# A 16-byte gap between the row tiles of the split weights in the feature-wise projections

## The chip, the cores and the metric

The kernel runs on one core of one Trainium2 chip. The metric is the device time of one execution in microseconds (us), here the median of three runs. All data are 32-bit floats. The core's engines are TensorE (PE in the profile; its weight loads stand apart as PEld), VectorE (DVE), ScalarE (ACT), GpSimd (POOL) and SyncE (SP, which here only starts transfers). SBUF is the on-chip memory, seen as 128 partitions; an address below is always a byte within a partition.

## The reference, cut to what matters

The program computes a two-layer encoder trunk for 256 tokens of width 2048. Each layer normalises its input, multiplies it by one wide input matrix, runs two groups of mixers on the parts (mLSTM and Mamba-2 in the first layer, sparse attention and gated delta rule in the second) and multiplies the result by an output matrix:

```python
D_MODEL, SEQ = 2048, 256
def layer_ab(x, norm_g, w_in, ..., w_out):
    h = rms_norm(x, norm_g)
    proj = jnp.einsum('btd,de->bte', h, w_in)          # the projections in question
    q, k, v, o_pre, z_a, i_pre, f_pre, z_b, xbc, dt_raw = split_cols(proj, SPLIT_AB)
    y_a = mlstm_branch(...)
    y_b = mamba2_branch(...)
    y = jnp.concatenate([y_a, y_b], axis=-1)
    return x + jnp.einsum('bte,ed->btd', y, w_out)
```

The second layer has the same form with other mixers. Most of the work is these matrix products with a weight that is read once from HBM.

## The kernel before, in words

**Three products for one.** A matrix is split into a rounded part and a rest: activations into `hi` and `lo`, weights into `wh` (a cast by ACT, line 254) and `wl` (raw weights minus `wh`, by DVE, line 255). A product is then `hi*wh + lo*wh + hi*wl`, three TensorE instructions in the one-pass type float32r that add up in one PSUM bank.

**Blocks of weights.** Weights come 512 columns wide, in groups of four row tiles of 128 rows (`KG = 4`). One transfer of 1 MB brings a group into a buffer `wr`; ACT and DVE split it in two halves of two row tiles each into `wh` and `wl` (`load_w`). In these buffers a row tile's 512 columns take 2048 bytes, and the next row tile follows at once: the four tiles of a group lie 2048 bytes apart. The buffers have 64 elements more than they need (`PAD`), and `SHIFT` says how many elements after the buffer's start the data begin: 8 or 24 for products with `hT`, 32 or 48 with `cT`, 0 with the units `ua`, `ub`, `uc`; the first of two is for token-wise, the second for feature-wise products.

**Two ways to multiply.** In `proj_tok` (tiles `pt`) the activations are the stationary operand and 512 weight columns stream past them. In `proj_feat` (tiles `pf`) the weights are the stationary operand, 128 columns at a time (block `b`), and 256 tokens stream past. The streamed operand is a row tile of `hT` (16 tiles of 512 elements: 256 `hi`, then 256 `lo`), or of `cT` for the products with `w_uk`. In the first three groups of a feature-wise projection the row tile `k` is the outer loop and the four blocks `b` the inner one, so 12 instructions use one row tile; in the last group it is the other way round, and the row tile changes every 3 instructions. A projection of 512 columns has 4 groups of 48 instructions; there are 36 of them with `hT`, and 4 of one group each with `cT`. Between row tiles `tick()` puts a few instructions of the mixers into TensorE's order.

**Places in SBUF.** In the built program every row tile of `hT` begins 192 bytes past a multiple of 256, and every row tile of `wh` and `wl` for a feature-wise product with `hT` begins on a multiple of 256. `cT` begins at 32 and its weights at 96. Take the start of the stationary operand minus the start of the streamed one, modulo 256, and call it the offset: it is 64 for all feature-wise products, in every row tile and block (blocks are 512 bytes apart, the `hi` and `lo` halves 1024). For all token-wise products it is 0. One other set of products matters below, the numerators `num` of the mLSTM heads: there `v` streams past `Ph` and `Pl`, 512 columns a time. `Ph` and `Pl` begin at 192; `v` begins at 192 in the even heads and at 96 in the odd ones, since the two are in different buffers. So the offset is 0 in even heads and 96 in odd ones.

Of the kernel before, what the change touches and what calls it, by code (L numbers as in the profile page):

```python
# [9 lines left out]
F32R = mybir.dt.float32r  # L10
# [19 lines left out]
KG, WR, WS = 4, 3, 2  # L30


PAD, SHIFT = 64, {"h": (8, 24), "c": (32, 48), "u": (0, 0)}


APART, APART_DG, APART_SP, SPARE = 56, 72, 72, 16
# [34 lines left out]
def trunk(ctx, tc, x, rel_bias, ab_norm, ab_w_in, ab_ml_b_i, ab_ml_b_f, ab_ml_norm, ab_ssm_conv_w,  # L71
# [21 lines left out]
    ab_w_in, ab_w_out, cd_w_in, cd_w_out = ab_w_in[0], ab_w_out[0], cd_w_in[0], cd_w_out[0]  # L93
# [4 lines left out]
    wp = ctx.enter_context(tc.tile_pool(name="wp", bufs=3))  # L98
# [12 lines left out]
    pin = tc.keep_in_program_order  # L111
# [80 lines left out]
    def pump():  # L192

        for gen in list(bg):
            if next(gen, "end") == "end":
                bg.remove(gen)
# [14 lines left out]
    def scaled_to(n):  # L211

        while scaling["done"] < n:
            next(scaling["gen"], None)
            scaling["done"] += 1

    def tick():

        if scaling["wait"] is not None and scaling["done"] < 8:
            scaling["wait"] -= 1  # L220
            if scaling["wait"] <= 0:
                scaled_to(scaling["done"] + 1)
                scaling["wait"] = 2
        ticking.append(True)
        beat[0] += 1
        for track in (steps, side):
            if track and (track is steps or not steps or beat[0] % 2) and next(track[0], "end") == "end":
                track.pop(0)
        ticking.clear()
# [8 lines left out]

    spare = []

    def load_w(src, r0, nk, pieces, n, shift, pin=lambda ins: ins, pool=None):


        pump()
        if spare:
            spare.append(spare.pop(0))
            pool = spare[0]
        wr = raw_w(src, r0, nk, pieces, n)
        wh, wl = parts_w(n, shift, pool)
        with tc.high_priority():  # L250
            m = nk // 2 if n == 512 else nk
            for k in range(0, nk, m):
                ks = slice(k, k + m)
                pin(A.copy(wh[:, ks, 0:n], wr[:, ks, 0:n]))  # L254
                pin(V.tensor_tensor(wl[:, ks, 0:n], wr[:, ks, 0:n], wh[:, ks, 0:n].bitcast(F32), op=OP.subtract))  # L255
        return wh, wl

    def raw_w(src, r0, nk, pieces, n, parts=None, after=()):

        wr = wp.tile([128, KG * 512], F32, name="wr", tag="wr", bufs=WR).rearrange("p (k n) -> p k n", n=n)  # L260
        if sum(m for _, m, _ in pieces) < n:
            G.memset(wr[:, 0:nk, 0:n], 0.0)
        k = 0
        for m in parts or [nk]:
            for c0, nc_, at in pieces:
                nc.sync.dma_start(wr[:, k:k + m, at:at + nc_], src[r0 + k * 128:r0 + (k + m) * 128, c0:c0 + nc_].rearrange("(k p) n -> p k n", p=128))
            k += m
            if after:
                after.pop()()
        return wr  # L270

    def parts_w(n, shift, pool=None):
        return [(pool or wp).tile([128, KG * 512 + PAD], F32R, name=name, tag=name, bufs=1 if spare and pool else WS)[:, shift:shift + KG * 512].rearrange("p (k n) -> p k n", n=n)
                for name in ("wh", "wl")]

    def token_part(pt, X, w, k, nk, t, cs, begun=False):
# [10 lines left out]
    def proj_tok(src, r0, X, c0, n=512, loads=(), begun=None):  # L287

        pts = begun or two_banks()
        nk = len(X)  # L290
        shift = SHIFT[X[0][0].name[0]][0]

        def part(pt, w, k, t):
            token_part(pt, X, w, k, nk, t, slice(0, n), begun and t == 0)

        for g in range(0, nk, KG):

            w = loads[g // KG] if loads else load_w(src, r0 + g * 128, KG, [(c0, n, 0)], n, shift)
            if g + KG == nk and not loads:
                order = [(k, t) for t in range(2) for k in range(KG)]  # L300
            else:
                order = [(k, t) for k in range(KG) for t in range(2)]
            for i, (k, t) in enumerate(order):
                part(pts[t], w, g + k, t)
                if i % 2:
                    tick()
        return pts

    def proj_feat(src, r0, X, pieces, loads=(), raw=False):


        n = max(p[2] + p[1] for p in pieces)
        n = (n + 127) // 128 * 128
        nb = n // 128
        pts = [ps.tile([128, 512], F32, name=f"pf{b}", tag="pt") for b in range((nb + 1) // 2)]
        nk = len(X)
        shift = SHIFT[X[0][0].name[0]][1]
        kg = KG * 512 // n
        for g, m in [(g, min(kg, nk - g)) for g in range(0, nk, kg)]:
            wh, wl = loads[g // kg] if g // kg < len(loads) else load_w(src, r0 + g * 128, m, pieces, n, shift)  # L320
            last = g + m == nk
            order = [(k, b) for b in range(nb) for k in range(m)] if last else [(k, b) for k in range(m) for b in range(nb)]
            for at, (k, b) in enumerate(order):
                xt, i = X[g + k]
                if xt is hT and not raw:
                    scaled_to(i // 2 + 1)
                bs = slice(b * 128, b * 128 + 128)
                pt = pts[b // 2][:, b % 2 * 256:b % 2 * 256 + 256]
                PE.matmul(pt, wh[:, k, bs], xt[:, i, 0:256], start=g + k == 0 and b % 2 == 0, stop=False)
                PE.matmul(pt, wh[:, k, bs], xt[:, i, 256:512], start=False, stop=False)  # L330
                PE.matmul(pt, wl[:, k, bs], xt[:, i, 0:256], start=False, stop=last and k == m - 1 and (b % 2 == 1 or b == nb - 1))
                if at % nb == nb - 1:
                    tick()
        return pts
# [144 lines left out]
    def first_input(pool, loads, c0, shift):  # L479
# [48 lines left out]
        def part(k, m):  # L528

            g, ks = k // 4, slice(k % 4, k % 4 + m)  # L530
            if len(loads) == g:
                loads.append(parts_w(512, shift))
            wh, wl = loads[g]
            with tc.high_priority():
                pin(A.copy(wh[:, ks], raw[g][:, ks]))  # L535
                pin(V.tensor_tensor(wl[:, ks], raw[g][:, ks], wh[:, ks].bitcast(F32), op=OP.subtract))  # L536
# [113 lines left out]
    with ExitStack() as st:  # L650
# [5 lines left out]
        pts = proj_tok(ab_w_in, 0, X, AV, loads=first_w, begun=begun)  # L656
        v_first = mp.tile([128, 2, 512], F32, name="v_first")
        bc_cols = lambda i: [(AXBC + 2048 + i * 512, 512, 0)]
        bc_w = [load_w(ab_w_in, 0, KG, bc_cols(0), 512, SHIFT["h"][1], pin)]
        for t in range(2):  # L660
            A.activation(v_first[:, t], pts[t], AF.Copy, scale=rs_x[:, t:t + 1])

# [5 lines left out]
        def bc_half(i):  # L668
            pts = proj_feat(ab_w_in, 0, X, bc_cols(i), () if i else bc_w)
            if not taps:  # L670
                taps.append(columns("xconv", [(rows(ab_ssm_conv_w[0, k]), 24) for k in range(4)] + [(rows(ab_ssm_conv_b[0]), 24)], mp, mp, nc.gpsimd))
            xconv = taps[0]
            for b in range(2):
                V.tensor_tensor(pair(pts[b]), pair(pts[b]), rb2, op=OP.mult)
                conv_gate(pts[b], xconv, 16 + i * 4 + b * 2, 24, xconv[:, 96:120], BC[:, i * 4 + b * 2:i * 4 + b * 2 + 2].rearrange("p b t -> p (b t)"))
# [88 lines left out]
        cd_ = dp.tile([4, 256], F32, name="cd_")  # L764
        ad_ = dp.tile([32, 256], F32, name="ad_")
        steps.append(gates(proj_feat(ab_w_in, 0, X, [(AI, 4, 0), (AFG, 4, 28), (ADT, 32, 32)])))
        bc_half(1)

        with sps:
# [107 lines left out]
            for g in range(4):  # L877

                pts = proj_feat(ab_w_in, 0, X, [(AXBC + g * 512, 512, 0)])
                flush()  # L880
                steps.extend(turns)
                turns.clear()
                xf = []
                for b in range(2):
                    xf.append(sp.tile([128, 512], F32, name="xf", tag="xf", bufs=2))
                    V.tensor_tensor(pair(pts[b]), pair(pts[b]), rb2, op=OP.mult)
                    conv_gate(pts[b], xconv, g * 4 + b * 2, 24, xconv[:, 96:120], xf[b])
                zb = sp.tile([128, 2, 512], F32, name="zb", tag="zb", bufs=ZB)
                gated = []
                steps.append(heads(g, xf, zb, gated, decays(g + 1) if g < 3 else lag(LE)))  # L890
                pts = proj_tok(ab_w_in, 0, X, AZB + g * 512)
                for t in range(2):
                    gate2(zb[:, t], pts[t], rsh[:, t:t + 1])
                gated.append(True)
# [143 lines left out]
    with ExitStack() as st:  # L1038
# [17 lines left out]
        for i in range(2):  # L1056
            pts = proj_feat(cd_w_in, 0, X, [(CIQ + i * 512, 512, 0)], raw=i == 0)
            for b in range(2):
                src = pair(pts[b])
                if i == 0:  # L1060
                    tm = kq.tile([128, 768], F32, name="tm", tag="tm", bufs=2)
                    src = tm[:, 0:512].rearrange("p (k t) -> p k t", k=2)
# [715 lines left out]
```

## Time and profile before

| | |
|---|---|
| median of 3 runs | 2044.75 us (2044.51 to 2045.87) |
| profiled execution, its own time | 2042.25 us |
| its span, first to last instruction | 2040.5 us |
| TensorE busy | 99% of the span, 13143 instructions |
| VectorE, ScalarE, GpSimd busy | 72%, 53%, 6% |
| TensorE's granted clock | 0.999 of full speed |
| chain that ended last | TensorE 98%: `pt` 47%, `pf` 40% |

A matmul's duration in the profile includes its way through the array, which overlaps with the next one: `pf` instructions last 280 ns but start about 113 ns after each other. So busy time tells little here, and the spacing from start to start is what counts. It is read from the timeline (start, duration, instruction, count) or from the chain of waits, whose pieces give a start, a length and a count: length over count is the time of one instruction.

### The profile page before, as it was taken

To read this page: it belongs to the slowest core of one execution; us is meant where nothing else is said; L and a number is where in the kernel's file an instruction comes from. 1 tells how busy PE (TensorE), PEld (TensorE's weight loads), DVE (VectorE), ACT (ScalarE), POOL (GpSimd) and SP (SyncE) were. 2 spreads that over 40 slices of the span, in tenths; PEclk is the share of its full clock that TensorE was granted. 3 is DMA by queue.
4 is the path that set the end of the run, shared out by engine and by line. 5 is a ranking of instruction groups with operands and counts; after the bars stand their busy time and mean duration, and the time that the engine had idled before them with its cause. 6 is when DMAs were issued, how large, how long until landed. Compare 5 with 4: busy or idle time off the path is not lost.

```text
span 2040.5 us, 32857 instructions
## 1 busy us (share of the span) xinstructions
PE 2027.8 (99%) x13143; PEld 1834.2 (90%) x13143; DVE 1478.2 (72%) x2459; ACT 1086.9 (53%) x1803; POOL 115.3 (6%) x188
## 2 busy tenths in 40 slices
PE   9999999999999999999999999999999999999998
PEld 8999998888889888999998888999999999999986
DVE  5998875555555566789699996556577767877776
ACT  6466644444434445567644444666466556555654
POOL 2000001000000000012210000000000000000001
PEclk9999999999999999999999999999999999999999
DMA  7655454656556565569966669565655555555543
GB/s 246 230 200 190 168 168 167 217 180 195 181 188 209 175 204 184 169 218 277 270 196 213 222 209 308 197 207 180 218 199 186 188 192 196 189 181 193 175 176 124
DMA packets 239434, 407.32 MB, mean 200 GB/s; under 512 B 42813, under 2 KB 68417, under 8 KB 238321
## 3 DMA queue, kind: packets, MB, share of 16 engines
q1 hardware_dynamic: 232432, 383.67, 56.5%
q0 software_dynamic: 4560, 18.15, 2.9%
q10 hardware_dynamic: 2288, 3.41, 0.5%
q8 instruction: 103, 1.69, 0.3%
q14 instruction: 51, 0.41, 0.1%
HBM read 388.26 MB, written 20.06 MB: 200 GB/s over the span
## 4 chain that ended last, share of the span: by engine, by line
PE 98%; DVE 1%; ACT 0%; DMA 0%; issue 0%; SPq 0%; DVEq 0%; ACTq 0%
PE pt L83 47%; PE pf L83 40%; PE pt_last L83 1%; PE py L83 1%; PE turn L87 1%; PE pu L83 1%; PE pog L83 1%; PE pq L83 1%; PE lgt L83 1%; PE po L83 1%; PE pn L83 0%; PE num L83 0%; DVE wl L255 0%; PE pw L83 0%; PE si L83 0%; PE xt L87 0%
## 5 line engine op out<-in xcount | busy, mean ns | idle before, releaser
L255 DVE TENSOR_TENSOR wl<-wr,wh 128x1024 fp32r<-128x1024 f32 x657 | 780.9, 1230 | 352.5 <-ACT wh L254 352.3
L254 ACT CAST wh<-wr 128x1024 fp32r<-128x1024 f32 x657 | 656.2, 1047 | 510.8 <-PE pt L83 253.7
L83 PE MATMUL pf<-hT,wh 128*128 128x256 f32 x4640 | 817.2, 280 | 0.0
L83 PEld LDWEIGHTS pf<-hT,wh 128*128 128x128 f32 x4640 | 704.5, 188 | 4.1 <-issue 1.9
L83 PE MATMUL pf<-hT,wl 128*128 128x256 f32 x2320 | 644.5, 278 | 0.0
L83 PE MATMUL pt<-wh,hT 128*128 128x512 f32 x1600 | 506.0, 392 | 0.0
L83 PEld LDWEIGHTS pf<-hT,wl 128*128 128x128 f32 x2320 | 436.5, 188 | 0.0
L83 PEld LDWEIGHTS pt<-wh,hT 128*128 128x128 f32 x1600 | 300.7, 188 | 61.9 <-ACT wh L535 0.5
L83 PE MATMUL pt<-wl,hT 128*128 128x512 f32 x800 | 312.4, 391 | 0.2 <-DVE wl L536 0.2
L83 PE MATMUL pt<-wh,uc 128*128 128x512 f32 x704 | 230.8, 399 | 0.0
L83 PEld LDWEIGHTS pt<-wl,hT 128*128 128x128 f32 x800 | 150.5, 188 | 31.0 <-DVE wl L536 1.5
L83 PEld LDWEIGHTS pt<-wh,uc 128*128 128x128 f32 x704 | 132.2, 188 | 25.9
L83 PE MATMUL pt<-wl,uc 128*128 128x512 f32 x352 | 138.2, 393 | 0.0
L637 DVE SCALAR_TENSOR_TENSOR cy<-pf,gconv,cy 128x255 f32<-128x255 f32 (+2 forms) x192 | 91.0, 479 | 7.8 <-ACT cy L633 5.0
L591 DVE TENSOR_TENSOR xr<-pt,xr 128x512 f32<-128x512 f32 x76 | 52.3, 688 | 41.5 <-PE pt L83 41.5
L83 PE MATMUL pt<-wh,ua 128*128 128x512 f32 x256 | 80.2, 393 | 0.0
L83 PE MATMUL pt<-wh,ub 128*128 128x512 f32 x256 | 79.2, 389 | 0.0
L83 PEld LDWEIGHTS pt<-wl,uc 128*128 128x128 f32 x352 | 66.4, 189 | 12.1
L83 PEld LDWEIGHTS pt<-wh,ub 128*128 128x128 f32 x256 | 48.1, 188 | 10.0
L83 PEld LDWEIGHTS pt<-wh,ua 128*128 128x128 f32 x256 | 47.9, 188 | 9.5
L633 ACT ACTIVATE cy<-pf,gconv 128x256 f32<-128x256 f32 x64 | 30.0, 469 | 47.2 <-DVE cy L637 35.6
L1576 POOL TENSOR_TENSOR QD<-QD,qm 128x256 f32<-128x256 f32 x32 | 27.2, 882 | 484.6 <-DVE qm L1571 275.2
(543 smaller groups left out, 2002.8 us busy)
## 6 DMA issues: line engine op xcount, KB each, us to landing
wr<-in_cd_w_in_dram SPq DMA_DIRECT2D x140, 1024.0 KB, 5.1
wr<-in_ab_w_in_dram SPq DMA_DIRECT2D x86, 1024.0 KB, 4.9
wr<-in_cd_w_out_dram SPq DMA_DIRECT2D x48, 1024.0 KB, 5.1
wr<-in_ab_w_out_dram SPq DMA_DIRECT2D x32, 1024.0 KB, 5.1
wr<-in_ab_w_in_dram SPq DMA_DIRECT2D x35, 512.0 KB, 4.5
zd<-zk SPq DMA_DIRECT2D x12, 512.0 KB, 6.7
Dt<-gd POOLq DMA_DIRECT2D x8, 512.0 KB, 6.4
wr<-in_cd_w_uk_dram SPq DMA_DIRECT2D x4, 1024.0 KB, 5.3
```

The source lines that it names most:

```text
L83: return held(nc.tensor.matmul(*args, **kw))
L87: return held(nc.tensor.transpose(*args, **kw))
L254: pin(A.copy(wh[:, ks, 0:n], wr[:, ks, 0:n]))
L255: pin(V.tensor_tensor(wl[:, ks, 0:n], wr[:, ks, 0:n], wh[:, ks, 0:n].bitcast(F32), op=OP.subtract))
L591: V.tensor_tensor(xc, pt, xc, op=OP.add)
L633: A.activation(yi, u, AF.Copy, scale=tap(3))
L637: V.scalar_tensor_tensor(yi[:, s:256], u[:, 0:256 - s], tap(3 - s), yi[:, s:256], op0=OP.mult, op1=OP.add)
L1576: G.tensor_tensor(QD[:, h], QD[:, h], qm[:, h // 2 * 256:h // 2 * 256 + 256], op=OP.mult)
```

## The change

Where a feature-wise projection is 512 columns wide, the row tiles of `wh` and `wl` are laid 516 elements apart instead of 512, by a new parameter `apart = 4` (16 bytes) of `load_w` and `parts_w`. Row tile 0 stays where it was; row tiles 1, 2 and 3 begin 16, 32 and 48 bytes later than before. The buffers keep their size (48 bytes fit into `PAD`) and their places, and no other tile moves. ACT's cast and DVE's subtraction now write two rows of 512 elements with a gap instead of 1024 in a row, and DVE reads `wh` so. The gate projection (128 columns wide), `proj_narrow` and all token-wise products keep their layout. Every engine's instructions stay in the same order; nothing is added, removed or moved.

```diff
-PAD, SHIFT = 64, {"h": (8, 24), "c": (32, 48), "u": (0, 0)}
+APART_K, PAD, SHIFT = 4, 64, {"h": (8, 24), "c": (32, 48), "u": (0, 0)}
...
-    def load_w(src, r0, nk, pieces, n, shift, pin=lambda ins: ins, pool=None):
+    def load_w(src, r0, nk, pieces, n, shift, pin=lambda ins: ins, pool=None, apart=0):
...
-        wh, wl = parts_w(n, shift, pool)
+        wh, wl = parts_w(n, shift, pool, apart)
...
-    def parts_w(n, shift, pool=None):
-        return [(pool or wp).tile([128, KG * 512 + PAD], F32R, name=name, tag=name, bufs=1 if spare and pool else WS)[:, shift:shift + KG * 512].rearrange("p (k n) -> p k n", n=n)
+    def parts_w(n, shift, pool=None, apart=0):
+        pitch = n + apart
+        return [(pool or wp).tile([128, KG * 512 + PAD], F32R, name=name, tag=name, bufs=1 if spare and pool else WS)[:, shift:shift + KG * 512 // n * pitch].rearrange("p (k n) -> p k n", n=pitch)[:, :, 0:n]
                 for name in ("wh", "wl")]
...
-            wh, wl = loads[g // kg] if g // kg < len(loads) else load_w(src, r0 + g * 128, m, pieces, n, shift)
+            wh, wl = loads[g // kg] if g // kg < len(loads) else load_w(src, r0 + g * 128, m, pieces, n, shift, apart=APART_K if n == 512 else 0)
...
-        bc_w = [load_w(ab_w_in, 0, KG, bc_cols(0), 512, SHIFT["h"][1], pin)]
+        bc_w = [load_w(ab_w_in, 0, KG, bc_cols(0), 512, SHIFT["h"][1], pin, apart=APART_K)]
```

## The prediction, made before the result

> **What bounds the kernel now.** I read the engines' shares and the chain of waits first.
>
> ```profile
> span 2040.5 us, 32857 instructions
> PE 2027.8 (99%) x13143; PEld 1834.2 (90%) x13143; DVE 1478.2 (72%) x2459; ACT 1086.9 (53%) x1803; POOL 115.3 (6%) x188
> PE 98%; DVE 1%; ACT 0%; DMA 0%; issue 0%; SPq 0%; DVEq 0%; ACTq 0%
> ```
>
> The chain that sets the end is TensorE for 98%, so only what changes the spacing of its instructions counts. The profiled execution took 2042.25 us, 1.75 us more than its span; the median is 2044.75 us, 4.25 us above the span. I work in the span and carry the difference over to the median.
>
> Next the chain in order of time, in its long unbroken pieces (start, us, what, count), and the timeline of one place:
>
> ```profile
> 1028.43 53.12 PE pf L83 x468
> 1081.55 174.10 PE pt L83 x768
> 1255.65 28.07 PE pf L83 x240
> 2008.94 22.08 PE pt_last L83 x120
> ```
>
> A feature-wise instruction costs 53.12/468 = 113.5 ns, a token-wise one 174.10/768 = 226.7 ns: twice the streamed columns, twice the time. So 113.3 ns is the pace of streaming 256 columns, and there is no room below it that the trace shows. But the piece at 1255.65 costs 28.07/240 = 117.0 ns. The timeline shows where its 192 instructions with `hT` (a whole projection) begin, where the 48 with `cT` begin, and what follows them:
>
> ```profile
> 1255.49 0.40 PE L83 MATMUL pf<-hT,wh 128*128 128x256 f32 x2
> ...
> 1278.10 0.41 PE L83 MATMUL pf<-cT,wh 128*128 128x256 f32 x2
> ...
> 1283.56 0.40 PE L83 MATMUL pt<-wh,cT 128*128 128x512 f32 x1
> ```
>
> The 192 go at 22.61/192 = 117.8 ns, the 48 at 5.46/48 = 113.8, with the same shape and offset (64). So feature-wise products know two paces, and can stay in one for a whole projection. The row of `pt_last` shows that the offset also plays a part: its 72 instructions of 512 columns at 226.7 ns take 16.3 us, which leaves 5.8 us for 48 of 256 columns at offset 0, or 120 ns each.
>
> How much time the slow pace takes now I counted from the starts of neighbouring `pf` instructions: of 6980 pairs, 5518 lie under 116 ns (mean 113.3), 1330 between 116 and 130 (mean 117.9), the rest have something between them. The first of the 1330 and the last:
>
> ```profile
> 33.11 0.40 PE L83 MATMUL pf<-hT,wh 128*128 128x256 f32 x2
> 33.35 0.28 PE L83 MATMUL pf<-hT,wl 128*128 128x256 f32 x1
> 33.47 0.40 PE L83 MATMUL pf<-hT,wh 128*128 128x256 f32 x2
> ...
> 1925.36 0.48 PE L83 MATMUL pf<-hT,wh 128*128 128x256 f32 x2
> 1925.68 0.28 PE L83 MATMUL pf<-hT,wl 128*128 128x256 f32 x1
> ```
>
> Three instructions from 33.11 to 33.47 are 0.36 us, 118 ns apiece after rounding. In all 1330 x (117.9 - 113.4) = 6.0 us: all that a better layout can win back.
>
> **The change part by part.** No instruction is added, removed or moved on any engine, so no wait, transfer or queue changes its place. Two things change: patterns that ACT and DVE write, and the offset between the operands of feature-wise products.
>
> *The patterns.* ACT's cast and DVE's subtraction write two rows of 512 instead of 1024 in one. The trace has no such pair with and without a gap at this size, but has one at half of it: `hT` is written as two rows of 256 with a gap of 256 (lines 424 and 423), `vf` as 512 in a row (lines 639 and 638).
>
> ```profile
> L255 DVE TENSOR_TENSOR wl<-wr,wh 128x1024 fp32r<-128x1024 f32 x656 | 778.6, 1228 | 348.6 <-ACT wh L254 348.3
> L639 DVE SCALAR_TENSOR_TENSOR vf<-vf,cy 128x512 f32<-128x512 f32 x16 | 11.0, 685 | 0.0
> L424 DVE TENSOR_TENSOR hT<-xg,hT 128x512 fp32r<-128x512 f32 x16 | 10.5, 688 | 0.9 <-ACT hT L423 0.9
> ...
> L254 ACT CAST wh<-wr 128x1024 fp32r<-128x1024 f32 x656 | 654.3, 1046 | 507.3 <-PE pt L83 253.7 <-PE pf L83 117.0 <-issue 94.9
> L638 ACT ACTIVATE vf<-cy 128x512 f32<-128x512 f32 x16 | 10.0, 627 | 6.0 <-DVE cy L637 6.0
> L423 ACT CAST hT<-xg 128x512 fp32r<-128x512 f32 x16 | 9.2, 618 | 8.8 <-DVE xg L436 5.6 <-DVE xg L462 3.1
> ```
>
> 688 against 685 ns on DVE, 618 against 627 on ACT: nothing, on the path or off it. Were it 5% (60 ns on each of 296 halves, 18 us on DVE), it would be hidden too: the 48 instructions of a group last 48 x 113.3 = 5.4 us, splitting the next group takes DVE 2 x 1.228 = 2.5 us and ACT 2.1, and ACT's idle time before its casts mostly ends when TensorE lets go of a buffer. With that cover gone it would be the 18 us.
>
> *The offset.* 37 times 192 = 7104 feature-wise instructions are 512 columns wide (`cT`'s included), 1776 for each row tile. Row tile 0 stays at offset 64, the others go to 80, 96 and 112. The trace has no row at 80 or 112, but it has 96: the numerators of the odd mLSTM heads, beside the even heads at offset 0, same instructions, same code. First two places of an odd head, then an even one:
>
> ```profile
> 325.11 0.63 PE L83 MATMUL num<-v,Ph 128*128 128x512 f32 x2
> 325.57 0.39 PE L83 MATMUL num<-v,Pl 128*128 128x512 f32 x1
> 325.80 0.40 PE L83 MATMUL pt<-wh,hT 128*128 128x512 f32 x1
> ...
> 327.17 0.63 PE L83 MATMUL num<-v,Ph 128*128 128x512 f32 x2
> 327.64 0.39 PE L83 MATMUL num<-v,Pl 128*128 128x512 f32 x1
> 327.87 0.63 PE L83 MATMUL num<-v,Ph 128*128 128x512 f32 x2
> 328.34 0.40 PE L83 MATMUL num<-v,Pl 128*128 128x512 f32 x1
> 328.58 0.39 PE L83 MATMUL pt<-wh,hT 128*128 128x512 f32 x1
> ...
> 454.52 0.62 PE L83 MATMUL num<-v,Ph 128*128 128x512 f32 x2
> 454.98 0.39 PE L83 MATMUL num<-v,Pl 128*128 128x512 f32 x1
> 455.20 0.62 PE L83 MATMUL num<-v,Ph 128*128 128x512 f32 x2
> 455.66 0.39 PE L83 MATMUL num<-v,Pl 128*128 128x512 f32 x1
> 455.88 0.39 PE L83 MATMUL pt<-wh,hT 128*128 128x512 f32 x1
> ```
>
> Odd: 0.69 us for 3 and 1.41 for 6, so 2.10/9 = 233.3 ns. Even: 1.36/6 = 226.7, exactly the pace of streaming. So offset 96 costs 6.6 ns on each instruction, though at 512 columns the weight load has twice its time. I take that for row tile 2: 1776 x 0.0066 = 11.7 us. Its bounds: the slow pace of `pf`, 117.8 - 113.3 = 4.5 ns (8.0 us), and the larger of the two odd stretches, 1.41/6 = 235.0, 8.3 ns (14.7 us).
>
> For row tiles 1 and 3 no row tells. Below, nothing excludes that they leave the slow pace for good (-0.9 ns each on average, 6.0 us over 6980); above, they can cost the 8.3 ns of the worst row. Offset 80 lies midway between 64 and 96, and 112 as far from 96 on the other side, so I take half of 6.6, 3.3 ns: 2 x 1776 x 0.0033 = 11.7 us. Row tile 0 I leave as it is. These prices are over the fast pace, and three quarters of the 6.0 us are paid there already: 11.7 + 11.7 - 4.5 = 18.9 us. Span 2040.5 + 18.9 = 2059.4; median 2044.75 + 18.9 = 2063.7, say **2064 us**.
>
> A rule speaks against all of this. The Trainium skill, page "TensorE: Matmul & The Clock Gate", section "Part 2: What happens when you issue a matmul", says that TensorE reads its streamed operand and its weights through two independent ports, so that loading the next weights takes no bandwidth from the running matmul. By that rule the sum would be 0 and the time 2044.75. The trace disagrees: 233.3 ns beside 226.7 for equal instructions whose operands lie differently.
>
> **The rivals.**
>
> *All three moved row tiles pay in full, and row tile 0 with them at times.* For it: the slow pace is kept once it is entered (192 instructions in the piece at 1255.65), and the change makes the offset jump every 12 instructions, every 3 in a last group. Against it: nothing is known at 80 and 112. Time: 3 x 1776 x 0.0066 - 4.5 = +30.7 us up to 3 x 1776 x 0.0083 + 1.5 = +45.7 us with the rest of row tile 0 slow at a quarter of the price: 2075 to 2090 us.
>
> *The jumps break the slow pace.* If a jump throws the reads out of step as well as into it, and no new offset has a price, the 6.0 us shrink: -4 to -6 us, 2039 to 2041 us. For it: in the piece at 1255.65 the slow pace ended as the next 48 instructions began with other tiles. It decides if 96 costs less than 6.0/1776 = 3.4 ns for 256 columns; the numerators' 6.6 stand against it. This is the case on the other side.
>
> *The offset does not matter for 256 columns*, as by that rule, or the price comes from `v` beginning 32 bytes off a multiple of 64, not from the offset. Against the latter: `cT` begins so too, and its 48 instructions in the piece at 1255.65 run at 113.8. Time: 2041 to 2048 us.
>
> *The change does not do what it says*: the pitch is seen in the built program's access patterns, row tiles 1 to 3 do begin 16, 32 and 48 bytes later; no chance is kept for this.
>
> **How the numbers follow.** The forecast (96 pays, 80 and 112 pay part) 0.43, with its own range 2052 to 2075: 8.0 us with nothing for the others is +6.5 once the 1.5 us already paid is taken off, 2051, rounded to 2052, and the first rival begins at 2075. All three in full 0.27; the slow pace broken 0.16; no matter 0.14. A measurement of this kernel tells about 0.2% (4.1 us) from no change. Faster by more than that needs at least 4.1 of the 6.0 us: 0.14, nearly all of that rival. Within it: the rest of it and the case without effect, 0.16. Slower: the first two, 0.70. The range reaches from the middle of the faster case, 2040, to the top of the first rival, 2090; about 0.15 is left outside, below and above together.
>
> **What would show it.** In the chain, pieces like the one at 1028.43 should cost 116 to 119 ns for each `pf` instruction in place of 113.5. Within a group of the timeline, the 12 instructions of row tile 2 should start some 120 ns apart, those of row tile 0 113; those of 1 and 3 are the open question. The mean of `pf` matmuls (280 and 278 ns now) should rise by a few ns, `pt` stay at 226.7 ns each, and the durations at lines 254 and 255 at 1046 and 1228 ns. I am wrong if row tile 2 runs at 113 ns, or if the chain gains pieces of DVE or ACT.

## The result and the profile after

The changed kernel takes 2068.39 us (median of 4 runs, 2068.23 to 2068.59) beside 2045.31 us of the kernel before (4 runs, 2044.51 to 2046.1): 23.1 us more, a ratio of 1.0114 with a 95% interval of 1.0102 to 1.0127. The profiled execution took 2068.59 us, its span is 2066.9 us: 26.4 more than the profiled span before, whose execution (2042.25 us) was one of the quick ones.

From the profile of the changed kernel, the span and engines, the chain of waits by engine, and the groups that matter, each shape by itself (busy, mean ns of one, idle time before):

```profile
span 2066.9 us, 32857 instructions
PE 2054.0 (99%) x13143; PEld 1860.3 (90%) x13143; DVE 1480.0 (72%) x2459; ACT 1089.6 (53%) x1803; POOL 114.2 (6%) x188
PE 97%; DVE 1%; DMA 1%; issue 0%; ACT 0%; SPq 0%; DVEq 0%; POOLq 0%; ACTq 0%
...
L255 DVE TENSOR_TENSOR wl<-wr,wh 128x1024 fp32r<-128x1024 f32 x656 | 778.5, 1228 | 366.0 <-ACT wh L254 364.6
L254 ACT CAST wh<-wr 128x1024 fp32r<-128x1024 f32 x656 | 654.9, 1046 | 551.1 <-PE pt L83 294.3 <-PE pf L83 133.8 <-issue 116.2
L83 PE MATMUL pf<-hT,wh 128*128 128x256 f32 x4640 | 843.8, 284 | 0.0
...
L83 PE MATMUL pf<-hT,wl 128*128 128x256 f32 x2320 | 652.4, 281 | 0.0
```

The chain is TensorE as before. DVE and ACT take 1228 and 1046 ns for a half, as before. These rows mix the 296 halves that now have a gap with 360 that have none; apart, ACT takes 1045 ns with a gap and 1047 without, DVE 1233 and 1224, so the gap costs at most 10 ns, off the chain. `pf` matmuls last 284 and 281 ns in place of 280 and 278.

The same pieces of the chain in order of time as in the prediction (start, us, what, count):

```profile
1042.40 55.44 PE pf L83 x468
1097.84 174.09 PE pt L83 x768
1271.93 28.43 PE pf L83 x240
```

The 468 feature-wise instructions now take 55.44/468 = 118.5 ns each, 113.5 before; the 768 token-wise ones 226.7 as before. The 240 that ran at 117.0, mostly at the slow pace, now take 118.5 too.

Inside one group, where each row tile serves 12 instructions, the timeline shows where the row tiles 0, 1, 2, 3 and then the next group begin:

```profile
1063.60 0.41 PE L83 MATMUL pf<-hT,wh 128*128 128x256 f32 x2
...
1064.99 0.40 PE L83 MATMUL pf<-hT,wh 128*128 128x256 f32 x2
...
1066.41 0.40 PE L83 MATMUL pf<-hT,wh 128*128 128x256 f32 x2
...
1067.84 0.40 PE L83 MATMUL pf<-hT,wh 128*128 128x256 f32 x2
...
1069.28 0.40 PE L83 MATMUL pf<-hT,wh 128*128 128x256 f32 x2
```

Row tile 0 takes 1.39/12 = 116 ns per instruction, the moved ones 118, 119 and 120. Over the whole program, from the starts of neighbouring `pf` instructions less than 130 ns apart, the means are:

| row tile (offset) | mean, ns | over the 114.24 of before | on 1776 instructions |
|---|---|---|---|
| 0 (64) | 116.86 | 2.62 | 4.7 us |
| 1 (80) | 118.85 | 4.61 | 8.2 us |
| 2 (96) | 118.25 | 4.01 | 7.1 us |
| 3 (112) | 119.04 | 4.80 | 8.5 us |

(The row of row tile 0 also holds 47 pairs of the gate projection.) That is 28.5 us, because each mean is set on all 1776 instructions; the 6848 pairs counted grew by 27.4 us together. All other intervals between TensorE's starts became 1.1 us shorter in sum, which leaves the 26.4 us of the span (26.3 from TensorE's first start to its last). Row tile 0, which did not move, is slower as well: a jump of the offset disturbs it. Where it has 12 instructions in a row, the first takes 121 ns on average and the fourth to the eleventh 115 to 116; in a projection's last group, where it has only three at a time, it never settles (119 ns in the group from 1046.58 us on).

### The profile page after: what moved, and what is told of

Its sections match the earlier page's. It is cut to its first block, busy times and chain, and to the rows that moved or that the text cites. A ratio compares the mean times of both kernels' runs of the same rounds, so it can differ in the third digit from the quotient of the medians.

```text
span 2066.9 us, 32857 instructions
## 1 busy us (share of the span) xinstructions
PE 2054.0 (99%) x13143; PEld 1860.3 (90%) x13143; DVE 1480.0 (72%) x2459; ACT 1089.6 (53%) x1803; POOL 114.2 (6%) x188
## 4 chain that ended last, share of the span: by engine, by line
PE 97%; DVE 1%; DMA 1%; issue 0%; ACT 0%; SPq 0%; DVEq 0%; POOLq 0%; ACTq 0%
PE pt L83 47%; PE pf L83 40%; PE pt_last L83 1%; PE py L83 1%; PE turn L87 1%; PE pu L83 1%; PE pog L83 1%; PE pq L83 1%; PE lgt L83 1%; PE po L83 1%; PE pn L83 0%; DMA U<-KUd 0%; PE num L83 0%; DMA xr<-in_x_dram 0%; PE si L83 0%; PE xt L87 0%
## 5 line engine op out<-in xcount | busy, mean ns | idle before, releaser
L83 PE MATMUL pf<-hT,wh 128*128 128x256 f32 x4640 | 843.8, 284 | 0.0
L83 PEld LDWEIGHTS pf<-hT,wh 128*128 128x128 f32 x4640 | 713.8, 189 | 4.1 <-issue 1.9
L83 PE MATMUL pf<-hT,wl 128*128 128x256 f32 x2320 | 652.4, 281 | 0.0
L1349 DVE TENSOR_TENSOR tmp<-U,Uw 128x62 f32<-128x62 f32 (+30 forms) x62 | 53.2, 858 | 1.6
```

The source lines that it names most:

```text
L83: return held(nc.tensor.matmul(*args, **kw))
L1349: V.tensor_tensor(tv, U[:, 0:s, s:s + 1].to_broadcast([128, s, n]), row.to_broadcast([128, s, n]), op=OP.mult)
```

## The experiments

Three questions: is it the offset or the gap, is it the offset or the place of the weights, and which offsets are good? For the first, the four row tiles lie next to each other as before and all start later by the same number of elements; for an offset beyond 112 or below 64 the start is taken modulo 64 elements (256 bytes), which is the same offset. The gate projection and the narrow one stay where they were. The edit to the kernel before, with the number for offset 80:

```diff
-PAD, SHIFT = 64, {"h": (8, 24), "c": (32, 48), "u": (0, 0)}
+MOVE, PAD, SHIFT = 4, 64, {"h": (8, 24), "c": (32, 48), "u": (0, 0)}
...
-        shift = SHIFT[X[0][0].name[0]][1]
+        shift = (SHIFT[X[0][0].name[0]][1] + (MOVE if n == 512 else 0)) % 64
...
-        bc_w = [load_w(ab_w_in, 0, KG, bc_cols(0), 512, SHIFT["h"][1], pin)]
+        bc_w = [load_w(ab_w_in, 0, KG, bc_cols(0), 512, (SHIFT["h"][1] + MOVE) % 64, pin)]
```

Each reading below shows the one piece of that kernel's chain that holds the same 468 feature-wise instructions (53.12 us before, 55.44 with the change). Each difference is against the kernel before as timed beside that run: 2042.93 us for 80, 96, 128 and 192, 2043.37 (one run) for 112, 0, 48 and 32, and 2044.57 for 68, 60 and the last two. The kernel before itself ranged from 2042.02 to 2047.04 us, and most of the variants ran once, so differences of less than some 5 us between them tell nothing.

**Offset 80** (`MOVE = 4`).

> All four row tiles of the 512-wide feature-wise products lie at offset 80 (the start is moved by 16 bytes, no gap between row tiles), so the offset never jumps. Grid theory (an offset that is not a multiple of 64 costs by itself): every one of 7104 instructions at the 119.0 ns that the changed kernel shows for row tile 1, 5.7 ns over 113.3, 40 us less the 6 us of slow pace that before pays already: about 2079 us. Jump theory (what costs is that the offset changes from row tile to row tile): no jumps, 2039 to 2048 us.

2070.64 us, +27.7.

```profile
1043.24 55.65 PE pf L83 x468
```

118.9 ns each, without any jump, and eight microseconds below the grid theory's number. The jump theory falls: most of the price is that of the offset itself.

**Offset 96** (`MOVE = 8`).

> All four row tiles at offset 96, no gap. Grid theory: 118.2 ns as row tile 2 shows, 4.9 x 7104 = 35 us less 6: about 2074 us. Jump theory: 2039 to 2048 us. If the numerators' price (6.6 ns) held here: 2086 us.

2068.07 us, +25.1; 117.5 ns each in the long piece.

```profile
1042.64 54.97 PE pf L83 x468
```

Six microseconds below the grid theory's number, eighteen below the one with the numerators' price. From all neighbours the mean is 118.1 ns, 4.8 over the pace of streaming: the price that the prediction had put at 6.6.

**Offset 128** (`MOVE = 16`).

> All four row tiles at offset 128, no gap. Grid theory: 128 is a multiple of 64, so 113.3 ns as at 64: 2039 to 2048 us, the slow pace more or less frequent. A third theory, that 64 itself is the one good place: about 5 ns on 7104, some 2075 us. Jump theory: 2039 to 2048 us.

2072.43 us, ratio 1.0143 (1.0127 to 1.0158), +29.5.

```profile
1043.40 56.22 PE pf L83 x468
```

120.1 ns. The grid theory, that multiples of 64 are good, falls with it.

**Offset 192** (`MOVE = 32`).

> All four row tiles at offset 192, no gap. Grid theory and jump theory: 2039 to 2048 us. The theory that 64 is the one good place: some 2075 us.

2059.59 us, ratio 1.0082 (1.0066 to 1.0099), +16.7: no theory's number.

```profile
1038.40 53.10 PE pf L83 x468
...
1265.60 28.27 PE pf L83 x240
```

This long piece is as fast as before, 113.5 ns, but the 240 behind it take 117.8 each. Over the whole program 81% of the neighbours are at 116 ns or more, against 19% at offset 64, while the two paces are nearly the same: means of 113.4 and 117.8 ns here, 113.3 and 117.9 there. So 192, which is 64 + 128, has the fast pace too, but is seldom in it.

**Offset 112** (`MOVE = 12`).

> All four row tiles at offset 112, no gap; it completes the set of the change's four offsets. Grid theory has fallen with offset 128 at 2072 us; the theory that stands is that every offset has a price of its own and 64 the lowest seen. The changed kernel's row tile 3 ran at 119.0 ns: 5.7 x 7104 = 40 less 6, +34 us if jumps cost nothing there; about +28 if, as at 80 (119.0 ns in the changed kernel, 118.6 alone), a part of it came from the jumps. So 2070 to 2078 us. If jumps cost nothing at all, the mean of the four (0, +27.7, +25.1 and this one) is the change's +23.1, which asks for +39.6 here: 2083 us.

2079.07 us, +35.7.

```profile
1047.50 56.22 PE pf L83 x468
```

Just above the range, and four microseconds below the number without any price of jumps. The four offsets of the change are now known alone: 0, +27.7, +25.1 and +35.7 us. Their mean is 22.1, and the change cost 23.1. By the traces, the pairs of neighbouring `pf` instructions under 130 ns grew by 0, 30.1, 26.4 and 38.1 us, a mean of 23.7, and under the change by 27.4. So the offsets make up most of the price, and the jumps 1 to 4 us in sum, which single runs cannot tell more closely. Part of what row tile 0 loses by them, others win back: row tile 3 ran at 119.0 ns in the changed kernel, while offset 112 alone has 119.8.

**Offset 0** (`MOVE = 48`).

> All four row tiles at offset 0, where token-wise products lie. The last 48 instructions of 256 columns of the kernel before (offset 0) go at 120 ns: 6.7 x 7104 = 47.6 less 6, about 2085 us. If what counts were only that the offset is small and positive, 2043 us.

2078.55 us, +35.2.

```profile
1047.58 56.21 PE pf L83 x468
```

120.1 ns, as the 48 instructions at the end of the kernel before had shown (120); the time is six microseconds below the forecast. The offset at which 512 columns run at their best pace seen (226.7 ns) is one of the worst for 256.

**Offset 48** (`MOVE = 60`).

> All four row tiles at offset 48, 16 bytes short of the place of before. If 64 is a narrow good place, some 5 ns each as at 80 and 96: 2068 to 2080 us. If the good offsets are a band that ends at 64: 2038 to 2048 us.

2068.51 us, +25.1: no band below 64.

```profile
1042.17 55.18 PE pf L83 x468
```

**Offset 32** (`MOVE = 56`).

> All four row tiles at offset 32. Narrow good place at 64: 2058 to 2080 us. A band below 64: 2038 to 2048 us; and if slow stretches are rarer there, down to 2037 us, the whole 6 us of slow pace gone.

2068.45 us, +25.1.

```profile
1042.23 55.43 PE pf L83 x468
```

**Offset 68** (`MOVE = 1`), one element beyond the place of before.

> All four row tiles at offset 68: one element beyond the place of before, no gap. So far 48 costs 25 us and 80 costs 28. If the price depends on the element, 68 is a step towards 80: about a quarter of it, +7 us, 2050 us. If only the 16-byte line counts in which a read begins, 68 is as 64: 2039 to 2048 us. If any start off a multiple of 16 bytes costs by itself: 2065 us or more.

2068.95 us, ratio 1.0120 (1.0104 to 1.0135), +24.4.

```profile
1042.23 55.44 PE pf L83 x468
```

Not a quarter of the price of 80, but nearly all of it, and the start is in the same 16 bytes as at 64. So the price does not grow with the way moved, and 68 is not as 64. What is left is the third case, a price of any start off a multiple of 16 bytes (2065 us or more), or a price of the offset that sets in with the first element; both are in keeping with this time. Moving both operands by one element would tell them apart, and no run does that.

**Offset 60** (`MOVE = 63`), one element short of it.

> All four row tiles at offset 60: one element short of the place of before. If the price depends on the element: a quarter of the way to 48, +6 us, 2049 us. If only the 16-byte line counts, 60 is as 48: 2068 us. If 64 is not the best place but only near it: below 2040 us.

2076.58 us, ratio 1.0157 (1.0140 to 1.0174), +32.0, more than at 48 and none of the three numbers.

```profile
1046.30 55.97 PE pf L83 x468
```

**Token-wise products at offset 96.** The numerators of the odd heads had carried the forecast. Are their 6.6 ns the offset's?

```diff
-PAD, SHIFT = 64, {"h": (8, 24), "c": (32, 48), "u": (0, 0)}
+MOVE, PAD, SHIFT = 40, 64, {"h": (8, 24), "c": (32, 48), "u": (0, 0)}
...
-        shift = SHIFT[X[0][0].name[0]][0]
+        shift = (SHIFT[X[0][0].name[0]][0] + MOVE) % 64
...
-        X, rs_x, rsh, rs16, rb, begun = first_input(mp, first_w, AV, SHIFT["h"][0])
+        X, rs_x, rsh, rs16, rb, begun = first_input(mp, first_w, AV, (SHIFT["h"][0] + MOVE) % 64)
```

> The token-wise products moved from offset 0 to 96, where the numerators of the odd heads lie; the feature-wise ones stay at 64. 4320 instructions of 512 columns. If the numerators' 6.6 ns is the price of the offset: 4320 x 0.0066 = 28.5 us, about 2072 us. If it belongs to the numerators alone (their other buffers, short runs of three): 2041 to 2050 us.

2071.34 us, +26.8 where 28.5 was expected. The long pieces of its chain:

```profile
1046.54 53.12 PE pf L83 x468
1099.66 179.93 PE pt L83 x768
```

The feature-wise piece is unchanged, the token-wise one takes 179.93/768 = 234.3 ns in place of 226.7: 7.6 ns more each. The rows of the numerators did measure the offset. (The feature-wise products, which were not touched, were at the slow pace in 27% of their neighbours here, 19% in the trace before: 2 us of the difference.)

**All places 32 bytes earlier, all offsets kept.** The identity matrix's tile is cut by eight unused elements, so that everything behind it moves:

```diff
-    ident = cp.tile([128, 64 + 128], F32, name="ident")[:, APART:APART + 128]
+    ident = cp.tile([128, 56 + 128], F32, name="ident")[:, APART:APART + 128]
```

> Every tile behind the identity matrix lies 32 bytes earlier, weights and activations alike, so every offset in the projections is as before and only the absolute places differ (the identity's own transposes excepted, some 350 of 13143 instructions). If the offset between the two operands is what counts: 2041 to 2048 us. If the weights' own place modulo 64 or 256 counts: as at offset 96 or 32, 2068 us.

2044.18 us, 0.4 below the kernel before.

```profile
1030.04 53.12 PE pf L83 x468
```

`hT` now begins at 160 and its weights at 224 modulo 256, instead of 192 and 0, and neither the time nor the long piece changes. (The slow pace takes 27% of the neighbours here too.) At offset 32 the weights begin at 224 as well, with `hT` at 192, and that run took 2068.45 us. So it is the offset between the two operands that counts, and not the weights' own place; this is shown for a move of 32 bytes, and no run moved both operands by less.

All offsets of the feature-wise products side by side (the first and the last row are the kernel before and the change):

| offset | change in time, us | ns each in the long piece |
|---|---|---|
| 64 | 0 | 113.5 |
| 0 | +35.2 | 120.1 |
| 32 | +25.1 | 118.4 |
| 48 | +25.1 | 117.9 |
| 60 | +32.0 | 119.6 |
| 68 | +24.4 | 118.5 |
| 80 | +27.7 | 118.9 |
| 96 | +25.1 | 117.5 |
| 112 | +35.7 | 120.1 |
| 128 | +29.5 | 120.1 |
| 192 | +16.7 | 113.5 |
| 64, 80, 96, 112 by row tile | +23.1 | 118.5 |

No layout that I tried beats the kernel before.

## Why the prediction was right, and which of its steps were not

**The bound** was read rightly. TensorE's pace sets the end, 97% of the chain after, and the whole loss lies in the spacing of the `pf` instructions.

**The patterns at nothing:** right, 1228 ns on DVE and 1046 on ACT before and after, and 1233 and 1045 for the halves with a gap alone.

**The offset has a price:** right, and this carried the sign. The steps behind it hold as well: the numerators' rows did measure the offset (token-wise products at 96: 7.6 ns each), and the place alone does nothing (everything moved by 32 bytes: -0.4 us in one run). The rule on the two independent ports (the Trainium skill, "TensorE: Matmul & The Clock Gate", "Part 2: What happens when you issue a matmul") would have given 2044.75 us; by 2068.39 us and 118.5 ns in place of 113.5 the trace does not agree with it for this type and these sizes.

**The sizes** were off in three terms, which cancel only in part. Over the pace of before:

| term | forecast, us | measured, us |
|---|---|---|
| row tile 2 (96): 11.7 less its third of 4.5 | 10.2 | 7.1 |
| row tiles 1 and 3 (80, 112): 11.7 less two thirds of 4.5 | 8.7 | 16.7 |
| row tile 0 (64) | 0 | 4.7 |
| all | 18.9 | 28.5; the pairs counted grew by 27.4, the span by 26.4 |

Row tile 2 was priced by instructions of 512 columns, 6.6 ns over the pace of streaming; at 256 columns the same offset costs 4.8 (offset 96 alone). Row tiles 1 and 3 were put halfway between two known offsets, at 3.3 ns. That step was wrong in kind: alone, 80 costs 5.3 ns, 96 costs 4.8 and 112 costs 6.5, so there is no slope from 64 to 96 to interpolate on. Row tile 0 was left as it was; the jumps take 2.6 ns from it. The median moved by 23.1 us, forecast 18.9; the profiled execution of before was one of its quickest, so its span makes the growth look 3 us larger than the medians do. So the sign and its cause were foreseen, but that the number came within 4.2 us is partly luck: one term too large made up for a quarter of two that were too small, and the medians grew 3 us less than the profiled pair.

**The rivals.** "All three in full, and row tile 0 at times" was right about the form: all moved row tiles pay about the same and row tile 0 pays a part. It was wrong about the price, which it took from the numerators (2075 to 2090 us); its upper sum also fails to take off the 4.5 us of slow pace that its lower one takes off. That the jumps would break the slow pace was wrong, though the trace shows the effect it spoke of: in the group from 1063.60 us on, row tile 0 comes to 113 to 115 ns after four or five instructions, only to be thrown out by the next jump. That the numerators' price comes from where `v` begins is ruled out by the run with all places 32 bytes earlier: there `v` of the odd heads begins at 64, a multiple of 64, and their instructions still start 233.3 ns apart, beside 226.7 in the even heads.

**Still open** is why 64 is good, why 192 is half so, and why moving by one element (68) costs nearly as much as moving by sixteen (128). The runs give the prices, no mechanism.

## What to carry to other kernels

Where one-pass 32-bit products with 256 streamed columns set the end, the place of the stationary operand relative to the streamed one is worth up to 6% of their pace, and it must be kept in every row tile: a gap that is harmless to the engines that write the tiles shifts this offset from tile to tile. Here a single element already cost 24 to 32 us. The price of an offset has to be measured at the shape in question, since 0 is the better of the two offsets measured for 512 columns and one of the worst for 256, and here it could not be interpolated between measured offsets. A trace of the kernel before often holds instructions of the same kind at another offset, like the numerators of odd and even heads here, and they give the sign before anything is tried.

## What I had not expected of the hardware

That a single element counts: at 68 the feature-wise products lose 24.4 us and at 60 they lose 32.0, while 64 loses nothing; whether by the offset itself or by a start off a multiple of 16 bytes is open. That 128 further on (192) the same fast pace exists, 113.5 ns over 468 instructions in a row, but is held by only 19% of the neighbours in the whole program, against 81% at 64. And that offset 0 (120.1 ns) costs 256 columns nearly 7 ns each, while 512 columns at the same offset run at 226.7 ns, twice the best pace of 256.
